# Feed-forward of a two-layer trunk: the first two feature tiles of each layer by eight plain products, their weights split ahead of the norm, a buffer for each feature tile

## The chip, the core and the metric

The kernel runs on one core of a Trainium2 chip. The metric is device time in microseconds of one execution, the median over runs. The engines are named as in the profile: PE (TensorE matmul), PEld (TensorE weight load), DVE (VectorE), ACT (ScalarE), POOL (GpSimd), SP (SyncE, which issues the loads spoken of here).

## The reference, cut to what matters

The program is one inference step of a two-layer trunk over 640 tokens of width 1024 (128 context tokens and 512 latent ones). Layer 0 mixes by attention and a state-space scan, layer 1 by an RWKV-7 scan. Behind each mixer stands the same feed-forward, which the change is about:

```
h = modulate(rmsnorm(x, P['norm_ffn_g'][layer]), sh2, sc2)
x = x + gt2 * swiglu(h, P['ffn_w_gate'][layer], P['ffn_w_up'][layer], P['ffn_w_down'][layer])
```

with `swiglu(h, wg, wu, wd) = (silu(h @ wg) * (h @ wu)) @ wd`. The hidden width is 2816, that is 22 feature tiles of 128. All of it is float32. The modulation (`sh2`, `sc2`, `gt2`) comes from a product of the condition vector with `mod_w`, which the kernel calls ada.

## The kernel before, in words

Both feed-forwards are made by one function, `ffn(layer, todo, keep, after)`. Tokens lie along the free axis, in two halves of 320; the width of 1024 lies on the partitions, in 8 blocks `k`.

**Precision.** Every product is made from operands split in a high part (a rounded cast, made on ACT) and a low part (the difference, made on DVE or POOL), by three matmuls: high by high, high by low, low by high. `operand(src)` splits 512 columns of weights: `S.copy` at L968 (tile `oh`), the subtraction on DVE at L969 (tile `ol`). Eight buffers of each are there.

**Seven products in place of eight.** For one feature tile, gate and up (2) by the two halves of the width (2) by the two halves of the tokens (2) would be 8 block products of 4 k-blocks, that is 12 matmuls of 128x320 each. The kernel uses a scheme with 7 (`PRODUCTS`), whose inputs are sums: on the side of the activations B11, B21, B22 and T1 to T4 (`sums`, each split in two steps of 640 columns), on the side of the weights four sums for each feature tile, made on POOL (`blocks`, L986, L987, L989, L991). Two feature tiles go together, a pair, so a pair has 2 x 7 x 12 = 168 matmuls (`product`, L1000). `collect` takes the results out of PSUM, adds, applies Silu and, in `to_hidden`, splits the hidden tile into `hid` (cast on ACT at L1009, low part on POOL at L1010).

**Order of the work.** The feature tiles go in groups of 4, 6, 6 and 6 (`GROUPS`). Behind each group come its down products (`down_step`, L1080). Ahead of the first pair stand the loads of its weights (SP), the splits of what is ready of them, two ada steps (`steps(jobs, 2)`: a load of 512 KB and 8 small matmuls each, L235), the sums of squares of the norm (L333), an inverse square root in 11 small DVE instructions (L117 to L123) and its spread over the partitions (`npr`, L347). Then `normed` makes h chunk by chunk (DVE at L1043, ACT at L1045). Within the first pair, each product is preceded by the making of its input.

**Memory.** All inputs h and later all hidden tiles share one buffer of 30,720 bytes a partition (`ip`, tag `hid`). Raw weights (6 of 4,096 bytes, shared with the ada loads), `oh` and `ol` (8 of 2,048 each) lie right behind it. A pool opened over memory that an earlier stage used waits, tile by tile, for the last use of what lay there. Ahead of the feed-forward of layer 0 stands the output projection (L401), whose weights take the first 36,864 bytes of this region and whose split inputs `mh` and `ml` the next 40,960; ahead of that of layer 1 stands the projection with `rwkv_w_o` (L1840). The order of instructions on an engine is made by a scheduler at build time, from the order in the program and its own estimates; on the chip each engine takes its instructions strictly in that order.

Of the kernel before, what the change touches and what calls it, by code (L numbers as in the profile page):

```python
# [18 lines left out]
NT = 640  # L19
# [69 lines left out]
def _build(ctx, tc, I, O):  # L89
# [863 lines left out]
    def ffn(layer, todo=(), keep=None, after=None):  # L953
        with ExitStack() as st, ExitStack() as hst:
            x = X[0]
            ip = pool(st, f"if{layer}")
            wp = pool(st, f"wf{layer}", 8)
            sqp = pool(st, f"sf{layer}", 10)
            pg = pool(st, f"pfg{layer}", 2, PSUM)
            pd = pool(st, f"pfd{layer}", 6, PSUM)  # L960
            jobs = [ada(l, p, wp, pg, "wr", 6, pg, "g") for l, p in todo]
            hf = ip.tile([128, 12, NT], F32, name="hf", tag="hid")

            def operand(src):

                hi = wp.tile([128, 512], F32R, name="oh", tag="oh")
                lo = wp.tile([128, 512], F32R, name="ol", tag="ol")
                S.copy(hi, src)  # L968
                V.tensor_tensor(out=lo, in0=src, in1=hi.bitcast(F32), op=ALU.subtract)  # L969
                return hi, lo  # L970

            def raw():
                return wp.tile([128, 1024], F32, name="wr", tag="wr", bufs=6)

            def blocks(f):
# [9 lines left out]
                g3 = wp.tile([128, 512], F32, name="g3", tag="g3", bufs=2)  # L985
                G.tensor_tensor(out=g3, in0=a11, in1=a21, op=ALU.add)  # L986
                G.tensor_tensor(out=a21, in0=a21, in1=a22, op=ALU.add)  # L987
                yield operand(a21)
                G.tensor_tensor(out=a11, in0=a11, in1=a21, op=ALU.add)  # L989
                yield operand(a11)  # L990
                G.tensor_tensor(out=a12, in0=a12, in1=a11, op=ALU.add)  # L991
                yield operand(a12)
                yield operand(g3)
                yield operand(a22)
# [8 lines left out]
            def piece():  # L1003
                return sqp.tile([128, 320], F32, name="e", tag="e")

            def to_hidden(e, slot, t0):

                hi, lo = hid[:, 2 * slot, t0:t0 + 320], hid[:, 2 * slot + 1, t0:t0 + 320]
                S.copy(hi, e)  # L1009
                G.tensor_tensor(out=lo, in0=e, in1=hi.bitcast(F32), op=ALU.subtract)  # L1010

            def collect(i, bank, e, slot):

                if i in (0, 2, 3):
                    e[i] = piece()
                    S.copy(e[i], bank[:, 0:320])
                elif i == 1:
                    e[1] = piece()
                    V.tensor_tensor(out=e[1], in0=bank[:, 0:320], in1=e[0], op=ALU.add)
                    S.activation(e[1], e[1], AF.Silu)  # L1020
                elif i == 4:
                    V.tensor_tensor(out=e[3], in0=bank[:, 0:320], in1=e[3], op=ALU.add)
                    S.activation(e[3], e[3], AF.Silu)
                else:
# [3 lines left out]
                    to_hidden(up, slot, 320 if i == 5 else 0)  # L1028
# [6 lines left out]
            H = {n: [hop.tile([128, 4, 320], F32R, name=n + z) for z in "hl"] for n, _, _ in PRODUCTS}  # L1035
            h = {f"B{a + 1}{b + 1}": hf[:, 4 * a:4 * a + 4, b * 320:b * 320 + 320] for a in range(2) for b in range(2)}
            h['T1'] = h['T3'] = hf[:, 8:10].rearrange("p a (b t) -> p (a b) t", b=2)
            h['T2'] = h['T4'] = hf[:, 10:12].rearrange("p a (b t) -> p (a b) t", b=2)

            def normed(a, half):  # L1040
                for k in range(4 * a, 4 * a + 4):
                    for v, c0, c1 in ((1, 320, 640),) if half else ((0, 0, 128), (1, 128, 320)):
                        V.scalar_tensor_tensor(out=hf[:, k, c0:c1], in0=x[:, k, c0:c1], scalar=ag[:, layer * 2 + 1, v, k:k + 1],  # L1043
                                               in1=rstd[v][:, c0 - 128 * v:c1 - 128 * v], op0=ALU.mult, op1=ALU.mult)
                        S.activation(hf[:, k, c0:c1], hf[:, k, c0:c1], AF.Identity, bias=mod[:, layer, v, 24 + k:25 + k])  # L1045

            def sums(n):

                if n in ('B11', 'B21'):
                    normed(n == 'B21', 0)  # L1050
                elif n in ('T1', 'T2'):
                    normed(n == 'T2', 1)
                for j in range(0, 4, 2):
                    js = slice(j, j + 2)
                    o = h[n][:, js]
                    if n == 'T1':
                        V.tensor_tensor(out=o, in0=h['B11'][:, js], in1=h['B12'][:, js], op=ALU.subtract)
                    elif n == 'T2':
                        V.scalar_tensor_tensor(out=o, in0=h['T1'][:, js], scalar=-1.0, in1=h['B22'][:, js], op0=ALU.mult, op1=ALU.subtract)
                    elif n == 'T3':  # L1060
                        V.tensor_tensor(out=o, in0=h['B22'][:, js], in1=h['B12'][:, js], op=ALU.subtract)
                    elif n == 'T4':
                        V.scalar_tensor_tensor(out=o, in0=h['T2'][:, js], scalar=-1.0, in1=h['B21'][:, js], op0=ALU.mult, op1=ALU.subtract)
                    S.copy(H[n][0][:, js], o)
                    (G if j else V).tensor_tensor(out=H[n][1][:, js], in0=o, in1=H[n][0][:, js].bitcast(F32), op=ALU.subtract)

            def down_blocks(f0, f1, q):

# [6 lines left out]

            def down_step(bank, c0, c1, ops, m, i, n):
                w = [o[:, (m % 4) * 128:(m % 4) * 128 + 128] for o in ops[i]]
                a = [hid[:, 2 * i + z, c0:c1] for z in range(2)]
                for z, (p, q) in enumerate(((w[0], a[0]), (w[0], a[1]), (w[1], a[0]))):
                    T.matmul(bank[:, 0:c1 - c0], p, q, start=i == 0 and z == 0, stop=i == n - 1 and z == 2)  # L1080

            for gi, (f0, f1) in enumerate(GROUPS):
                n = f1 - f0
                for fp in range(f0, f1, 2):
                    gens = first if fp == 0 else [blocks(f) for f in (fp, fp + 1)]
                    banks, es = [{}, {}], [{}, {}]
                    for i, (hn, b, start) in enumerate(PRODUCTS):
                        ops = early[i] if fp == 0 and i < 2 else [next(g) for g in gens]
                        if fp == 0 and i < 6:
                            sums(hn)  # L1090
                            if i == 5:
                                sums('T4')
                                hid = ip.tile([128, 12, NT], F32R, name="hid", tag="hid")
# [812 lines left out]
```

## Time and profile before

| | us |
|---|---|
| median of 3 runs | 2154.29 |
| lowest and highest run | 2151.95, 2156.15 |
| profiled execution, its own time | 2159.76 |
| its span, first to last instruction | 2158.0 |
| PE busy in the span | 1965.2 (91%) |
| DVE, ACT, POOL busy | 1461.4, 947.4, 684.1 |
| feed-forward of layer 0: first product, first product of the second pair | at 456.25, at 497.55 |
| feed-forward of layer 1: the same | at 1692.78, at 1733.88 |

The profiled execution was 5.5 us longer than the median of the runs. Its span leaves out 1.8 us around it. The mean granted clock of TensorE in the span was 0.934.

### The profile page before, as it was taken

To read this page: it belongs to the slowest core of one execution; us is meant where nothing else is said; L and a number is where in the kernel's file an instruction comes from. 1 tells how busy PE (TensorE), PEld (TensorE's weight loads), DVE (VectorE), ACT (ScalarE), POOL (GpSimd) and SP (SyncE) were. 2 spreads that over 40 slices of the span, in tenths; PEclk is the share of its full clock that TensorE was granted. 3 is DMA by queue.
4 is the path that set the end of the run, shared out by engine and by line. 5 is a ranking of instruction groups with operands and counts; after the bars stand their busy time and mean duration, and the time that the engine had idled before them with its cause. 6 is when DMAs were issued, how large, how long until landed. Compare 5 with 4: busy or idle time off the path is not lost. (4 is left out here: it accounts for less than half of the span.)

```text
span 2158.0 us, 42969 instructions
## 1 busy us (share of the span) xinstructions
PE 1965.2 (91%) x17653; PEld 1791.4 (83%) x17653; DVE 1461.4 (68%) x2527; ACT 947.4 (44%) x1738; POOL 684.1 (32%) x596
## 2 busy tenths in 40 slices
PE   7999988978999999989999897877889699999998
PEld 6887776968999999969676786866778589999998
DVE  4474675377665757587676839989766876666575
ACT  4333454253443524356555243544553634444351
POOL 2112231044442426131144123314231545345340
PEclk8999899979999999989997988878789799999999
DMA  8663001134342424242466635434243242223221
GB/s 293 212 214 99 3 1 40 40 117 128 94 151 79 148 65 131 105 131 64 129 220 211 214 100 140 123 90 148 81 148 92 85 127 78 81 63 113 59 89 50
DMA packets 256408, 245.73 MB, mean 114 GB/s; under 512 B 27849, under 2 KB 217298, under 8 KB 256084
## 3 DMA queue, kind: packets, MB, share of 16 engines
q1 hardware_dynamic: 233076, 208.87, 32.1%
q0 software_dynamic: 5856, 21.01, 3.0%
q10 hardware_dynamic: 17280, 13.11, 2.0%
q8 instruction: 139, 2.28, 0.5%
q14 instruction: 57, 0.47, 0.1%
HBM read 203.76 MB, written 39.19 MB: 113 GB/s over the span
## 5 line engine op out<-in xcount | busy, mean ns | idle before, releaser
L969 DVE TENSOR_TENSOR ol<-wr,oh 128x512 fp32r<-128x512 f32 x352 | 344.0, 991 | 110.6 <-ACT oh L968 101.3
L968 ACT CAST oh<-wr 128x512 fp32r<-128x512 f32 x352 | 216.4, 619 | 327.8 <-PE d L1080 187.5
L1080 PE MATMUL d<-hid,oh 128*128 128x320 f32 x1312 | 290.6, 310 | 5.4 <-POOL hid L1010 5.4
L1080 PEld LDWEIGHTS d<-hid,oh 128*128 128x128 f32 x1312 | 220.5, 189 | 5.9 <-POOL hid L1010 5.9
L1080 PE MATMUL d<-hid,ol 128*128 128x320 f32 x656 | 203.4, 310 | 0.0
L443 DVE SCALAR_TENSOR_TENSOR x<-d,mod,x 128x128 f32<-128x128 f32 (+2 forms) x204 | 77.3, 434 | 167.5 <-PE d L1080 133.3
L1010 POOL TENSOR_TENSOR hid<-e,hid 128x320 fp32r<-128x320 f32 x88 | 102.1, 1174 | 141.7 <-ACT hid L1009 138.7
L986 POOL TENSOR_TENSOR g<-wr 128x512 f32<-128x512 f32 x44 | 62.8, 1427 | 261.9 <-DMA wr<-in_ffn_w_up_dram 222.1
L401 PE MATMUL d<-hh,wh 128*128 128x320 f32 (+1 forms) x464 | 119.0, 328 | 6.2 <-ACT hh L435 3.6
L1080 PEld LDWEIGHTS d<-hid,ol 128*128 128x128 f32 x656 | 123.8, 189 | 0.0
L401 PE MATMUL d<-hl,wh 128*128 128x320 f32 (+1 forms) x464 | 115.4, 320 | 3.9 <-POOL hl L436 3.9
L401 PE MATMUL d<-hh,wl 128*128 128x320 f32 (+1 forms) x464 | 114.1, 318 | 0.6 <-DVE wl L388 0.6
L388 DVE TENSOR_TENSOR wl<-wr,wh 128x1024 fp32r<-128x1024 f32 (+1 forms) x57 | 70.6, 1239 | 55.2 <-ACT wh L386 54.7
L386 ACT CAST wh<-wr 128x1024 fp32r<-128x1024 f32 (+1 forms) x57 | 58.7, 1034 | 104.3 <-PE d L401 71.7
L401 PEld LDWEIGHTS d<-hh,wh 128*128 128x128 f32 (+1 forms) x464 | 79.9, 191 | 20.8 <-ACT hh L435 5.0
L989 POOL TENSOR_TENSOR wr<-wr 128x512 f32<-128x512 f32 x44 | 63.5, 1446 | 82.7 <-DVE ol L969 57.2
L1009 ACT CAST hid<-e 128x320 fp32r<-128x320 f32 x88 | 40.5, 460 | 110.0 <-DVE e L1027 109.8
L991 POOL TENSOR_TENSOR wr<-wr 128x512 f32<-128x512 f32 x44 | 67.9, 1554 | 63.7 <-DVE ol L969 63.6
L401 PEld LDWEIGHTS d<-hl,wh 128*128 128x128 f32 (+1 forms) x464 | 80.3, 191 | 7.7 <-POOL hl L436 5.2
L401 PEld LDWEIGHTS d<-hh,wl 128*128 128x128 f32 (+1 forms) x464 | 80.2, 191 | 2.7 <-DVE wl L388 1.2
L1489 PE MATMUL pS<-ar,ta 64*128 64x128 f32 x640 | 57.1, 314 | 19.6 <-POOL uv L1557 7.6
L1489 PEld LDWEIGHTS pS<-ar,ta 64*128 64x128 f32 x640 | 49.2, 216 | 26.8 <-POOL ar L1476 8.9
(606 smaller groups left out, 6037.2 us busy)
## 6 DMA issues: line engine op xcount, KB each, us to landing
wt<-in_mod_w_dram SPq DMA_DIRECT2D x80, 512.0 KB, 4.4
wr<-in_ffn_w_gate_dram SPq DMA_DIRECT2D x44, 512.0 KB, 4.0
wr<-in_ffn_w_up_dram SPq DMA_DIRECT2D x44, 512.0 KB, 4.6
wr<-in_ffn_w_down_dram SPq DMA_DIRECT2D x44, 512.0 KB, 4.5
ta<-kbd SPq DMA_DIRECT2D x10, 1024.0 KB, 6.5
ar<-rkd SPq DMA_DIRECT2D x20, 512.0 KB, 6.3
wr<-in_ab_w_in_dram SPq DMA_DIRECT2D x16, 512.0 KB, 8.5
wt<-in_mod_w_dram SPq DMA_DIRECT2D x6, 1024.0 KB, 10.5
```

Of the source, the lines that this page charges most:

```text
L386: S.copy(wh, wr)
L388: V.tensor_sub(wl, wr, wh.bitcast(F32))
L401: T.matmul(ps[b][0:cn, 0:320], w[:, k, 0:cn], a[:, t0:t1], start=(k == 0 and i == 0), stop=(k == w.shape[1] - 1 and i == 2))
L443: V.scalar_tensor_tensor(out=x[:, k, c0:c1], in0=ps[b][:, c0 - 320 * b:c1 - 320 * b], scalar=mod[:, layer, v, gcol + k:gcol + k + 1], in1= ...
L968: S.copy(hi, src)
L969: V.tensor_tensor(out=lo, in0=src, in1=hi.bitcast(F32), op=ALU.subtract)
L986: G.tensor_tensor(out=g3, in0=a11, in1=a21, op=ALU.add)
L989: G.tensor_tensor(out=a11, in0=a11, in1=a21, op=ALU.add)
L991: G.tensor_tensor(out=a12, in0=a12, in1=a11, op=ALU.add)
L1010: G.tensor_tensor(out=lo, in0=e, in1=hi.bitcast(F32), op=ALU.subtract)
L1080: T.matmul(bank[:, 0:c1 - c0], p, q, start=i == 0 and z == 0, stop=i == n - 1 and z == 2)
L1489: T.matmul(pS[i][:, m], bk[r, g4 * 4 + m, :], ar[r, g4 * 4 + m], start=True, stop=True)
```

## The change

For feature tiles 0 and 1 of each layer the eight plain block products take the place of the seven: no sums of weights are needed, and no T1 to T4. So all eight weight operands of the two tiles are split before the norm. The products run k by k: as soon as one block of 320 tokens is normed and split (`normed`, `part_of`), its matmuls follow (`plain_step`); first the first half of the tokens for both tiles, then the second half. T1 to T4 are made behind that, for the later pairs. The second pair (tiles 2 and 3) makes its weight sums on DVE in place of POOL, and the last pair of each group makes the low parts of its hidden tiles on DVE in place of POOL. The one buffer for h and hidden tiles becomes six of [128, 4, 320]; some of the H tiles, the raw weights and the operands get places of their own, in another order of pools in each layer. Four ada steps stand in the first pair (two behind each half) where three stood.

```diff
-            ip = pool(st, f"if{layer}")
+            if layer == 0:
+                ip, sqp = pool(st, "if0", 6), pool(st, "sf0", 11)
+                hops.update(dict.fromkeys(('B11', 'B21', 'T1'), pool(st, "hf0a")))
+                gp, wrp = pool(st, "gf0", 2), pool(st, "wr0", 6)
+            else:
+                wrp, ip, sqp = pool(st, "wr1", 6), pool(st, "if1", 6), pool(st, "sf1", 11)
+                hops.update(dict.fromkeys(('B22', 'T2', 'T3', 'T4'), pool(st, "hf1a")))
+                gp = pool(st, "gf1", 2)
             wp = pool(st, f"wf{layer}", 8)
-            sqp = pool(st, f"sf{layer}", 10)
...
+                if plain:
+                    yield operand(a21)
+                    yield operand(a22)
+                    return
...
-            first = [blocks(f) for f in (0, 1)]
-            early = [[next(g) for g in first] for _ in range(2)]
+            first = [list(blocks(f, True)) for f in (0, 1)]
             steps(jobs, 2)
             rstd = norm_spread(norm_rstd(pg, sqp), pd, "d")
...
+            for half in range(2):
+                at = [('B11', 'B21'), ('T4', 'B22')][half]
+                ps = [[pd.tile([128, 512], F32, name="d", tag="d") for _ in range(2)] for f in range(2)]
+
+                def plain_step(f, k):
+                    for i in range(2):
+                        w, a = first[f][2 * i + k // 4], H[at[k // 4]]
+                        jw = slice((k % 4) * 128, (k % 4) * 128 + 128)
+                        for z, (p, q) in enumerate(((w[0], a[0]), (w[0], a[1]), (w[1], a[0]))):
+                            T.matmul(ps[f][i][:, 0:320], p[:, jw], q[:, k % 4], start=k == 0 and z == 0, stop=k == 7 and z == 2)
+
+                for k in range(8):
+                    n = f"B{1 + k // 4}{1 + half}"
+                    normed(n, k % 4)
+                    part_of(n, slice(k % 4, k % 4 + 1), at[k // 4])
+                    plain_step(0, k)
+                    if not half:
+                        plain_step(1, k)
+                if half:
+                    for k in range(8):
+                        plain_step(1, k)
+                for f in range(2):
+                    e = piece()
+                    S.activation(e, ps[f][0][:, 0:320], AF.Silu)
+                    V.tensor_tensor(out=e, in0=ps[f][1][:, 0:320], in1=e, op=ALU.mult)
+                    to_hidden(e, f, half, V)
+                steps(jobs, 2)
+            for n in ('T1', 'T2', 'T3', 'T4'):
+                sums(n)
...
-                for fp in range(f0, f1, 2):
-                    gens = first if fp == 0 else [blocks(f) for f in (fp, fp + 1)]
+                for fp in range(max(f0, 2), f1, 2):
+                    gens = [blocks(f, E=V if fp == 2 else G) for f in (fp, fp + 1)]
...
-                            collect(i, banks[z][b], es[z], fp - f0 + z)
+                            collect(i, banks[z][b], es[z], fp + z, V if fp + 2 == f1 else G)
```

`part_of(n, js)` casts a piece of h to the high part on ACT and subtracts on DVE; `sums(n)` makes one of T1 to T4 on DVE in two steps of 640 columns and calls it for each.

## Rows read from the trace of the kernel before

**Rows 1.** The page: busy us of each engine and its share.

```profile
PE 1965.2 (91%) x17653; PEld 1791.4 (83%) x17653; DVE 1461.4 (68%) x2527; ACT 947.4 (44%) x1738; POOL 684.1 (32%) x596
```

**Rows 2.** The chain that ended last, a piece of it: start us, us, what.

```profile
1910.32 74.00 PE d L1000 x504
```

**Rows 3.** Stretches: length; busy us (instructions) PE, PEld, DVE, ACT, POOL; clock, DMA.

```profile
434.14:456.25 22.11, 11.11 (x65) 8.01 (x65) 16.69 (x35) 8.64 (x20) 12.53 (x8) 0.61 0.48 141
456.25:497.55 41.30, 33.98 (x177) 30.48 (x177) 36.74 (x45) 27.62 (x55) 23.47 (x15) 0.83 0.30 87
497.55:524.71 27.16, 27.16 (x196) 25.34 (x195) 22.69 (x35) 13.91 (x29) 10.03 (x9) 1.00 0.58 177
524.71:555.70 30.99, 28.41 (x194) 28.15 (x193) 17.79 (x33) 5.79 (x10) 12.57 (x10) 1.00 0.11 34
...
1672.10:1692.78 20.68, 9.01 (x66) 6.64 (x65) 15.61 (x34) 8.16 (x19) 10.04 (x7) 0.67 0.33 103
1692.78:1733.88 41.10, 34.33 (x177) 29.50 (x177) 36.52 (x45) 27.52 (x55) 23.52 (x14) 0.83 0.29 87
...
1761.15:1793.93 32.78, 29.95 (x194) 29.68 (x193) 18.19 (x33) 5.79 (x10) 12.84 (x11) 0.95 0.11 30
```

**Rows 4.** PE in order of time ahead of the first product, layer 0, then layer 1.

```profile
439.74 1.08 PE L235 MATMUL pa<-wt,sT 128*32 128x256 f32 x8 [5.61 <-DMA wt<-in_mod_w_dram]
...
451.18 2.47 PE L347 MATMUL npr<-ca,rs 128*128 128x128 f32 x10 [4.57 <-DVE rs L123]
...
1675.21 0.64 PE L235 MATMUL pa<-wt,sT 128*32 128x256 f32 x8 [3.11 <-DMA wt<-in_mod_w_dram]
...
1676.02 1.25 PE L333 MATMUL nps<-ca,acc 128*128 128x1 f32 x10
1677.14 2.27 PE L333 MATMUL nps<-ca,sq 128*128 128x1 f32 x10
...
1687.71 2.48 PE L347 MATMUL npr<-ca,rs 128*128 128x128 f32 x10 [7.29 <-DVE rs L123]
```

**Rows 5.** DVE in order of time ahead of the first product, layer 0.

```profile
445.39 2.88 DVE L969 TENSOR_TENSOR ol<-wr,oh 128x512 fp32r<-128x512 f32 x2 [1.81 <-ACT oh L968]
448.20 0.15 DVE L117 TENSOR_SCALAR rq_v<-nps 128x5 f32<-128x5 f32 x1
...
453.70 2.49 DVE L1043 SCALAR_TENSOR_TENSOR hf<-x,ag,npr 128x192 f32<-128x192 f32 x8 [0.84 <-PE npr L347]
```

**Rows 6.** SP: issues of the first weight loads, layer 0 (first, last) and layer 1.

```profile
427.13 0.37 SPq L103 DMA_DIRECT2D wr<-in_ffn_w_gate_dram  x1
...
433.29 0.37 SPq L103 DMA_DIRECT2D wr<-in_ffn_w_up_dram  x1
...
1663.51 0.37 SPq L103 DMA_DIRECT2D wr<-in_ffn_w_gate_dram  x1
```

**Rows 7.** ACT in order of time ahead of the first product, layer 0.

```profile
444.74 1.14 ACT L968 CAST oh<-wr 128x512 fp32r<-128x512 f32 x2 [5.92 <-POOL wr L987]
...
454.14 1.44 ACT L1045 ACTIVATE hf<-hf,mod 128x192 f32<-128x192 f32 x4 [0.79 <-DVE hf L1043]
```

**Rows 8.** Groups by line: weight splits without POOL beside them, in the first pair; copies there.

```profile
L969 DVE TENSOR_TENSOR ol<-wr,oh 128x512 fp32r<-128x512 f32 x3 | 2.1, 694 | 0.1
...
L969 DVE TENSOR_TENSOR ol<-wr,oh 128x512 fp32r<-128x512 f32 x7 | 10.1, 1457 | 0.0
...
L1016 ACT COPY e<-d 128x320 f32<-128x320 f32 x6 | 2.6, 428 | 5.7 <-PE d L1000 5.7
```

**Rows 9.** PE in order of time at the first down products, layers 0 and 1.

```profile
531.11 0.41 PE L1080 MATMUL d<-hid,oh 128*128 128x320 f32 x1 [2.58 <-POOL hid L1010]
...
1767.81 0.42 PE L1080 MATMUL d<-hid,oh 128*128 128x320 f32 x1 [2.83 <-POOL hid L1010]
```

**Rows 10.** PE in order of time in the first pair, at the low clock.

```profile
478.06 0.47 PE L1000 MATMUL d<-T2l,oh 128*128 128x320 f32 x1
478.33 0.47 PE L1000 MATMUL d<-T2h,ol 128*128 128x320 f32 x1
```

More of the change, by code (lines that the diff above doesn't have):

```diff
@@ L955, in ffn, with hid_tile @@
             x = X[0]
-            ip = pool(st, f"if{layer}")
+            hops = {}
+            if layer == 0:
[6 more added lines that the diff above has]
+                gp = pool(st, "gf1", 2)
             wp = pool(st, f"wf{layer}", 8)
-            sqp = pool(st, f"sf{layer}", 10)
             pg = pool(st, f"pfg{layer}", 2, PSUM)
             pd = pool(st, f"pfd{layer}", 6, PSUM)
-            jobs = [ada(l, p, wp, pg, "wr", 6, pg, "g") for l, p in todo]
-            hf = ip.tile([128, 12, NT], F32, name="hf", tag="hid")
+            jobs = [ada(l, p, wrp, pg, "wr", 6, pg, "g") for l, p in todo]
+            def hid_tile(dt):
+                return ip.tile([128, 4, 320], dt, name="hid", tag="hid")
             def operand(src):
@@ L972, in raw, with blocks @@
             def raw():
-                return wp.tile([128, 1024], F32, name="wr", tag="wr", bufs=6)
-            def blocks(f):
+                return wrp.tile([128, 1024], F32, name="wr", tag="wr")
+            def blocks(f, plain=False, E=G):
                 ws = []
@@ L984, in blocks @@
                 yield operand(a12)
-                g3 = wp.tile([128, 512], F32, name="g3", tag="g3", bufs=2)
-                G.tensor_tensor(out=g3, in0=a11, in1=a21, op=ALU.add)
-                G.tensor_tensor(out=a21, in0=a21, in1=a22, op=ALU.add)
+                if plain:
+                    yield operand(a21)
+                    yield operand(a22)
+                    return
+                g3 = gp.tile([128, 512], F32, name="g3", tag="g3")
+                E.tensor_tensor(out=g3, in0=a11, in1=a21, op=ALU.add)
+                E.tensor_tensor(out=a21, in0=a21, in1=a22, op=ALU.add)
                 yield operand(a21)
-                G.tensor_tensor(out=a11, in0=a11, in1=a21, op=ALU.add)
+                E.tensor_tensor(out=a11, in0=a11, in1=a21, op=ALU.add)
                 yield operand(a11)
-                G.tensor_tensor(out=a12, in0=a12, in1=a11, op=ALU.add)
+                E.tensor_tensor(out=a12, in0=a12, in1=a11, op=ALU.add)
                 yield operand(a12)
@@ L1004, in piece, with to_hidden, collect @@
                 return sqp.tile([128, 320], F32, name="e", tag="e")
-            def to_hidden(e, slot, t0):
-                hi, lo = hid[:, 2 * slot, t0:t0 + 320], hid[:, 2 * slot + 1, t0:t0 + 320]
+            hid = {}
+            def to_hidden(e, f, b, E):
+                if f not in hid:
+                    hid[f] = hid_tile(F32R)
+                hi, lo = hid[f][:, b], hid[f][:, 2 + b]
                 S.copy(hi, e)
-                G.tensor_tensor(out=lo, in0=e, in1=hi.bitcast(F32), op=ALU.subtract)
-            def collect(i, bank, e, slot):
+                E.tensor_tensor(out=lo, in0=e, in1=hi.bitcast(F32), op=ALU.subtract)
+            def collect(i, bank, e, f, E):
                 if i in (0, 2, 3):
@@ L1034, in ffn, with part_of, normed @@
             hop = pool(hst, f"hf{layer}", 1, side="right")
[L1035 to L1045, printed above, removed]
+            H = {n: [hops.get(n, hop).tile([128, 4, 320], F32R, name=n + z) for z in "hl"] for n, _, _ in PRODUCTS}
+            h = {n: hid_tile(F32) for n in ('B11', 'B21', 'B12', 'B22', 'T2')}
+            h.update(T1=h['B11'], T3=h['B12'], T4=h['T2'])
+            def part_of(n, js, out=None):
+                hi, lo = (z[:, js] for z in H[out or n])
+                S.copy(hi, h[n][:, js])
+                V.tensor_tensor(out=lo, in0=h[n][:, js], in1=hi.bitcast(F32), op=ALU.subtract)
+            def normed(n, j):
+                k, half = j + 4 * (n[1] == '2'), n[2] == '2'
+                for v, c0, c1 in ((1, 320, 640),) if half else ((0, 0, 128), (1, 128, 320)):
+                    o = h[n][:, j, c0 - 320 * half:c1 - 320 * half]
+                    V.scalar_tensor_tensor(out=o, in0=x[:, k, c0:c1], scalar=ag[:, layer * 2 + 1, v, k:k + 1],
+                                           in1=rstd[v][:, c0 - 128 * v:c1 - 128 * v], op0=ALU.mult, op1=ALU.mult)
+                    S.activation(o, o, AF.Identity, bias=mod[:, layer, v, 24 + k:25 + k])
             def sums(n):
[L1049 to L1052, printed above, removed]
                 for j in range(0, 4, 2):
@@ L1056, in sums @@
                     if n == 'T1':
-                        V.tensor_tensor(out=o, in0=h['B11'][:, js], in1=h['B12'][:, js], op=ALU.subtract)
+                        V.tensor_tensor(out=o, in0=o, in1=h['B12'][:, js], op=ALU.subtract)
                     elif n == 'T2':
@@ L1060, in sums @@
                     elif n == 'T3':
[L1061 to L1065, printed above, removed]
+                        V.tensor_tensor(out=o, in0=h['B22'][:, js], in1=o, op=ALU.subtract)
+                    else:
+                        V.scalar_tensor_tensor(out=o, in0=o, scalar=-1.0, in1=h['B21'][:, js], op0=ALU.mult, op1=ALU.subtract)
+                    part_of(n, js)
+            for half in range(2):
[25 more added lines that the diff above has]
+                sums(n)
             def down_blocks(f0, f1, q):
@@ L1077, in down_step @@
                 w = [o[:, (m % 4) * 128:(m % 4) * 128 + 128] for o in ops[i]]
-                a = [hid[:, 2 * i + z, c0:c1] for z in range(2)]
+                a = [hid[f0 + i][:, 2 * z:2 * z + 2].rearrange("p b t -> p (b t)")[:, c0:c1] for z in range(2)]
                 for z, (p, q) in enumerate(((w[0], a[0]), (w[0], a[1]), (w[1], a[0]))):
@@ L1083, in ffn @@
                 n = f1 - f0
-                for fp in range(f0, f1, 2):
-                    gens = first if fp == 0 else [blocks(f) for f in (fp, fp + 1)]
+                for fp in range(max(f0, 2), f1, 2):
+                    gens = [blocks(f, E=V if fp == 2 else G) for f in (fp, fp + 1)]
                     banks, es = [{}, {}], [{}, {}]
                     for i, (hn, b, start) in enumerate(PRODUCTS):
[L1088 to L1093, printed above, removed]
+                        ops = [next(g) for g in gens]
                         for z in range(2):
```

2 lines of the change are left out of this document (1 added, 1 removed).

## The prediction

> **What bounds the kernel now.** I read the page first: PE is busy for 91% of the span [rows 1], so time can only come off where PE waits, runs at the lower clock, or does less. The chain of waits then shows where it does none of the first two: most of each feed-forward is an unbroken run of products, 504 of them in 74.00 us, which makes 0.147 us a matmul of 128x320 [rows 2]. A pair of 168 is 24.7 us at that rate, and the second pair of layer 0 takes 27.16 us with its three ada steps [rows 3]: nothing is to be had there. The table of stretches says what is left. From the end of the projection to the first product PE is busy for 11.11 of 22.11 us in layer 0 and 9.01 of 20.68 us in layer 1; the first pair takes 41.30 and 41.10 us at a mean clock of 0.83; the first group of down products takes 30.99 and 32.78 us for 192 matmuls that need 28.2 [rows 3]. These three places, in two layers, are all that the change touches.
>
> Last I asked each engine what it waits for there. Ahead of the first product of layer 0, PE waits 5.61 us for the load of an ada weight and then 4.57 us for the inverse square root on DVE; in layer 1 the two waits are 3.11 and 7.29 us [rows 4]. The ada loads are late because they stand in SP's queue behind four weight loads, and those start only at 427.13 to 433.29 and at 1663.51 [rows 6], while the projection ends at 434.14 and 1672.10: their buffers lie over that projection's operands. The root is late because DVE, which takes its queue in order, has weight splits ahead of it that wait for ACT casts, which wait for sums on POOL: 5.92 us on ACT [rows 7], then two splits at 445.39 and only at 448.20 the root [rows 5]. In layer 1 PE is through with the squares at 1679.4, and the spread, which needs the root, starts at 1687.71 [rows 4].
>
> **The norm stretch.** By the sizes of the pools, the raw weights of layer 0 come to lie 79,680 bytes into the region, behind the 77,824 that the projection uses. Their loads and all eight splits can be done beside the projection, where PE alone is busy. The POOL sums are gone. PE in layer 0: projection to 434.14; two ada steps at 0.64 [rows 4] to 435.4; the accumulated squares 1.25 at the full clock, the last ones 2.27 at the half clock [rows 4], with 0.2 for the opening matmul: 439.1. The root took 2.98 from its start to the spread, the spread 2.47 [rows 4, 5]: 444.5. From the end of the spread to the first product it was 2.6 before, with four blocks and a cast of 640 columns ahead; now it is one block: DVE 0.31, ACT 0.36 [rows 5, 7], a cast near the 0.43 of a 320 copy [rows 8], 0.2 of handing on: 1.3. First product at 445.8 in place of 456.25: **10.5 us**. In layer 1 the raw weights lie over the scan's buffers and load early, but most of `oh` lies over the last projection slabs, so I let all eight splits wait for its end: 8 x 0.69 [rows 8] from about 1673.5 is 1679.0, which is later than PE's squares (1677.0). Then 2.98 + 2.48 + 1.3: 1685.7 in place of 1692.78, **7.1 us**. Bounds: 5.6 and 3.1 less if the loads still come late; 2 more in layer 1 if the splits come early.
>
> **The first pair.** It gets 24 matmuls more, 192 x 0.147 = 28.2 us, and four ada steps, 2.6. Will it be fed? A block of 320 tokens costs DVE two chunks of 0.31 and a subtraction of about 0.45 (320 columns, by the 0.69 that 512 take [rows 8]), together 1.1 us, and ACT about 1.1; its 12 matmuls take 1.76. So PE sets the pace in the first half and DVE and ACT run ahead by some 5 us for the second, where a block costs about 1.0 us for 0.88 us of the first tile's matmuls, and the second tile's 7 us follow without any need. T1 to T4 (16 DVE steps of 640 columns, about 0.86, 13.8 us) come behind that, under the second half's 14.1. The clock had a mean of 0.61 and 0.67 ahead of the first product, 0.83 in the pair and 1.00 behind it [rows 3], and at the half level a product takes 0.27 [rows 10]. I allow 4 us at the half level, which costs 2.0, and 1.5 for the first blocks and for the change of halves, where PSUM banks come free. Sum 34.3, against 41.30 and 41.10: **7.0 and 6.8 us**. Bounds: 30.8 with no such loss; with the whole first half at 0.27 (96 x 0.12 = 11.8 in place of 2.0) 44.1, a loss of 3.
>
> The Trainium skill ("TensorE: Matmul & The Clock Gate", Part 1) says that the array's default state is the throttled one and that steady work releases it. By it, matmuls added right behind a wait are the dearest in the kernel, and the first rival below is how far that could go; if both halves ran so, the pair would take about 55 us. The 0.83 of the old pair, with its waits, agrees in kind; a pair without them should come up sooner, and I stay with 4 us.
>
> **The second pair.** Its weight operands need buffers that the plain products free one by one: after the first tile's block 4 of the second half, two, some 10 us before the pair begins. DVE was busy for 22.7 of 27.2 us there [rows 3]; it gets 8 sums of 0.69 and 4 low parts of 0.5, 7.5 us, and loses the delay that POOL's work beside it gave: the same split takes 0.69 without POOL and 1.46 in the first pair with it [rows 8]. With 10.03 us of POOL work gone from that stretch I take the two as equal: 0. Bounds: 3 us a layer lost if the delay stays, 8 if T1 to T4 come late as well.
>
> **The first down products.** PE waits 2.58 and 2.83 us for a low part on POOL [rows 9], and in layer 1 the stretch falls to a clock of 0.95 [rows 3]. On DVE the low part takes 0.5 and does not queue behind POOL's sums of the next pair. From the last product it takes two DVE steps, a cast and that, 1.9 us alone and 3.3 at the slow rate; 24 matmuls cover 3.5. So the excess of 2.8 and 4.6 nearly goes: **6.5 us**. For the other groups 48 matmuls cover it already, and POOL against DVE makes no odds. If DVE is queued up: 3.
>
> **Ada.** Four steps in the first pair in place of three leave one less for later in each layer: **1.3 us**. The six buffers for hidden tiles, the extra one of 11 for `e` and the new order of pools cost nothing by themselves: hidden tile 1 may have to wait for an input tile to come free, but is read only 30 us later.
>
> **Sum.** 10.5 + 7.1 + 7.0 + 6.8 + 6.5 + 1.3 = 39.2 us. The profiled execution took 2159.76, so 2120.6; it was 5.5 above the median of the runs, and the prediction is for that: **2115**.
>
> **Rivals.** *The first half stays at the low clock.* The rows show the clock falling again within the first pair (0.83). If gaps between blocks keep it down for all 96 products, each layer loses 9.8: 2135. Against it: 12 matmuls a block on 1.1 us of supply. *The second pair runs short of operands*, DVE having T1 to T4, the sums and the low parts at once: 8 each, 2131. For it: DVE was busy for 36.7 of 41.3 us in the first pair. *The change doesn't bring the loads forward*, the scheduler leaving them behind the projection: 5.6 + 3.1 lost, 2124. *DVE becomes the bound, and the kernel is slower.* The place is from the norm to the end of the second pair. DVE had 59 us of work there [rows 3] and gets 7 subtractions at 0.86 that POOL had and 8 sums at 0.69: 71 if nothing gets faster, against 61.5 of PE. It decides from 81 us a layer, where the 39 are used up; at 85 the time is 2162. Against it: POOL has next to nothing left there.
>
> *The busiest engine's work decides.* 48 matmuls more on PE are 48 x 0.147 = 7.0 us, and if the waits only moved, the time would be 2161. The Trainium skill ("Perfetto Trace Analysis", Identifying the Most-Contended Engine) says to look to the engine with the highest occupancy first, which is PE here, and by it work should not be added there. The rows speak against it: PE is idle for 11 us ahead of each first product.
>
> **How the numbers follow.** My forecast, a gain of 30 to 48 us: 0.70. Low clock 0.08, second pair 0.09, late loads 0.08, DVE as the bound 0.03, more PE work 0.02. All but the last two are faster. A time within 0.2% (4.3 us, what a measurement of this kernel can tell from no change) fits none of them well; I leave 0.03 for it, 0.04 for slower, 0.93 for faster. Without any stall or loss of clock the gain would be 49, so 2105; above, the range takes in the late loads, the second pair and half of the low clock's cases: 2104 to 2134.
>
> **What would show it.** The first weight loads issued long before the projection's end; no wait of PE for an ada load; the first product 10.5 and 7 us earlier; 192 products in some 32 us with the clock back within the first 5; the second pair starting at 479 to 480 where it was 497.55 and taking 27 us or less; no wait for a low part at the first down products. The prediction is wrong if the product stretch shows waits for DVE, if the second pair takes over 30 us, or if the spread still waits for splits.

## The result, and the profile after

The changed kernel takes 2119.89 us (median of 4 runs, 2116.96 to 2125.63) against 2155.22 before (4 runs): a ratio of 0.9841, interval 0.9815 to 0.9866. That is 35.3 us off. The forecast was 2115, with a range of 2104 to 2134: faster, as predicted, at nearly the predicted size. Two of its terms were wrong all the same, and the experiments below are about those.

The profiled execution took 2116.96 us, the fastest of the four. The page's first row answers to [rows 1]:

```profile
PE 1950.7 (92%) x17701; PEld 1785.1 (84%) x17701; DVE 1447.0 (68%) x2589; ACT 940.2 (44%) x1734; POOL 560.6 (27%) x510
```

PE has 48 matmuls more and is busy for 14.5 us less; the mean granted clock of the span is 0.943 where it was 0.934. The table of stretches, cut at the same four places as [rows 3] (end of the projection, first product, second pair, first down product, next pair), layer 0 and then layer 1; columns as there:

```profile
429.14:439.37 10.23, 8.46 (x82) 5.46 (x81) 5.55 (x24) 3.26 (x10) 0.00 (x0) 0.83 0.83 222
439.37:475.83 36.46, 33.59 (x219) 32.12 (x219) 26.78 (x55) 22.55 (x52) 0.00 (x0) 0.91 0.19 68
475.83:501.62 25.79, 24.90 (x170) 24.64 (x169) 24.75 (x42) 16.44 (x33) 2.62 (x2) 1.00 0.45 123
501.62:533.67 32.05, 30.30 (x194) 29.64 (x193) 20.08 (x38) 5.97 (x11) 8.43 (x7) 0.95 0.11 34
1645.53:1658.54 13.01, 10.77 (x80) 6.44 (x80) 10.32 (x31) 7.34 (x18) 0.00 (x0) 0.61 0.76 232
1658.54:1692.81 34.27, 31.62 (x216) 30.69 (x213) 26.40 (x55) 22.27 (x52) 0.00 (x0) 0.95 0.30 96
1692.81:1718.60 25.79, 24.90 (x170) 24.64 (x169) 24.75 (x42) 16.48 (x33) 2.53 (x2) 1.00 0.44 123
1718.60:1749.60 31.00, 29.13 (x195) 28.25 (x194) 20.11 (x38) 5.99 (x11) 8.85 (x7) 1.00 0.12 35
sum 208.60, PE 193.67 PEld 181.88 DVE 158.75 ACT 100.29 POOL 22.43; mean PE 24.21 PEld 22.73 DVE 19.84 ACT 12.54 POOL 2.80
```

The same eight stretches took 243.4 us before, so they give 34.8 of the 35.3. The spans of the two profiled executions differ by 8 us more; that lies outside these stages (5.0 ahead of layer 0's, 4.5 between the layers, 1.5 the other way behind), and in the runs below these outer parts moved by about as much from one execution to the next. Set beside the forecast, in us saved over both layers:

| term | forecast | measured |
|---|---|---|
| norm stretch | 10.5 + 7.1 = 17.6 | 11.9 + 7.7 = 19.6 |
| first pair | 7.0 + 6.8 = 13.8 | 4.8 + 6.8 = 11.6 |
| second pair, with the ada term | 1.3 | 1.4 + 1.5 = 2.9 |
| first down products | 6.5 | -1.1 + 1.8 = 0.7 |
| sum | 39.2 | 34.8 |

**Norm stretch.** The loads and PE in order of time, layer 0 (SP's first issue of a feed-forward weight and its last of an ada weight there, then PE), which answer to [rows 6] and [rows 4]; the last two rows are PE in layer 1:

```profile
369.58 0.71 SPq L103 DMA_DIRECT2D wr<-in_ffn_w_gate_dram  x1
...
391.05 1.81 SPq L103 DMA_DIRECT2D wt<-in_mod_w_dram  x2
...
430.47 1.25 PE L333 MATMUL nps<-ca,acc 128*128 128x1 f32 x10
431.59 1.25 PE L333 MATMUL nps<-ca,sq 128*128 128x1 f32 x10
432.77 3.60 PE L235 MATMUL pa<-wt,sT 128*32 128x256 f32 x32
436.30 1.38 PE L347 MATMUL npr<-ca,rs 128*128 128x128 f32 x10
439.37 1.25 PE L1096 MATMUL d<-B11h,oh 128*128 128x320 f32 x4 [1.69 <-ACT B11h L1060]
...
1652.60 1.08 PE L235 MATMUL pa<-wt,sT 128*32 128x256 f32 x8 [1.56 <-DMA wt<-in_mod_w_dram]
1654.09 2.48 PE L347 MATMUL npr<-ca,rs 128*128 128x128 f32 x10 [0.41 <-DVE rs L123]
```

The first weight load is issued 60 us before the projection ends at 429.14, where it was 7 us [rows 3, 6]. In layer 0 no wait for an ada load is left, and the wait for the root has gone: four ada steps fill it. Their loads still stand behind the four weight loads in SP's queue, but that whole queue is now issued ahead of the projection's end. The spread took 1.38, where [rows 4] had 2.47. In layer 1 a wait of 1.56 us for an ada load is left, in time in which the root is not ready either, then 0.41 for the root, and 0.27 for another ada load just ahead of the first product; the spread takes 2.48.

**Change of halves.** PE at the end of the first half of the first pair, layer 0 and layer 1:

```profile
455.18 1.07 PE L235 MATMUL pa<-wt,sT 128*32 128x256 f32 x16
456.80 0.44 PE L243 MATMUL pm<-ca,mr 128*128 128x128 f32 x2 [0.55 <-DVE mr L240]
459.56 0.64 PE L235 MATMUL pa<-wt,sT 128*32 128x256 f32 x8 [2.32 <-DMA wt<-in_mod_w_dram]
...
1677.09 0.85 PE L1096 MATMUL d<-T4h,oh 128*128 128x320 f32 x4 [2.10 <-ACT T4h L1060]
```

The last product of the first half ends near 455.2, and the first of the second starts at 460.13: 4.88 us without one, 4.21 in layer 1. `T4h` holds the high part of the second half's first inputs here. Behind the gap come products at 0.27 us each, the half level, and the second half's 96 products take 15.7 us in both layers in place of 14.1. DVE at that place, layer 0, and ACT's first cast for the second half:

```profile
454.48 0.49 DVE L1111 TENSOR_TENSOR e<-d,e 128x320 f32<-128x320 f32 x1 [6.62 <-ACT e L1110]
455.36 0.49 DVE L1111 TENSOR_TENSOR e<-d,e 128x320 f32<-128x320 f32 x1 [0.39 <-ACT e L1110]
456.32 0.42 DVE L240 COPY mr<-pa 128x256 f32<-128x256 f32 x1 [0.47 <-PE pa L235]
456.66 0.88 DVE L1028 TENSOR_TENSOR hid<-e,hid 128x320 fp32r<-128x320 f32 x2
457.46 1.92 DVE L1067 SCALAR_TENSOR_TENSOR hid<-x,ag,npr 128x320 f32<-128x320 f32 x4
...
458.96 0.80 ACT L1060 CAST T4h<-hid 128x320 fp32r<-128x320 f32 x2
```

DVE has nothing to do for 6.62 us. Then it collects the first half's result into the two hidden tiles (L1111, L1028), and only behind that makes the first input of the second half (L1067). It did not run ahead. In layer 1 PE starts 0.5 us behind the start of the first cast of `T4h`, for which it waits. In layer 0 that cast starts at 458.96 and PE at 460.13, so of layer 0's gap the ada step of 459.56 can account for some 0.7 us at most.

**First down products.** PE, then DVE and POOL just before, layer 0; [rows 9] is the place before:

```profile
506.55 0.41 PE L1130 MATMUL d<-hid,oh 128*128 128x320 f32 x1 [1.25 <-ACT hid L1027]
507.46 0.41 PE L1130 MATMUL d<-hid,oh 128*128 128x320 f32 x1 [0.50 <-DVE hid L1028]
...
499.12 1.59 DVE L1045 SCALAR_TENSOR_TENSOR e<-e 128x320 f32<-128x320 f32 x1
500.63 1.77 DVE L979 TENSOR_TENSOR ol<-wr,oh 128x512 fp32r<-128x512 f32 x1
502.32 1.57 DVE L1028 TENSOR_TENSOR hid<-e,hid 128x320 fp32r<-128x320 f32 x1
...
504.22 1.38 DVE L979 TENSOR_TENSOR ol<-wr,oh 128x512 fp32r<-128x512 f32 x1
...
498.92 1.43 POOL L1000 TENSOR_TENSOR g<-wr 128x512 f32<-128x512 f32 x1 [142.84 <-DVE e L1044]
500.43 1.42 POOL L1001 TENSOR_TENSOR wr<-wr 128x512 f32<-128x512 f32 x1
502.23 1.32 POOL L1000 TENSOR_TENSOR g<-wr 128x512 f32<-128x512 f32 x1 [0.38 <-DMA wr<-in_ffn_w_up_dram]
```

The low part is on DVE now, but POOL's sums for the next pair run at the same moment: three DVE steps that take 0.48 to 0.69 elsewhere take 1.6 to 1.8, and a weight split of the next pair (L979, at 504.22) takes 1.38 between the last steps of the hidden tiles.

### The profile page after: what moved, and what is told of

Its sections match the earlier page's. It is cut to its first block, busy times and chain, and to the rows that moved or that the text cites. A ratio compares the mean times of both kernels' runs of the same rounds, so it can differ in the third digit from the quotient of the medians.

```text
span 2115.2 us, 42931 instructions
## 1 busy us (share of the span) xinstructions
PE 1950.7 (92%) x17701; PEld 1785.1 (84%) x17701; DVE 1447.0 (68%) x2589; ACT 940.2 (44%) x1734; POOL 560.6 (27%) x510
## 5 line engine op out<-in xcount | busy, mean ns | idle before, releaser
L979 DVE TENSOR_TENSOR ol<-wr,oh 128x512 fp32r<-128x512 f32 x344 | 316.1, 935 | 101.0 <-ACT oh L978 93.6
L978 ACT CAST oh<-wr 128x512 fp32r<-128x512 f32 x344 | 211.3, 619 | 307.1 <-PE d L1130 174.7
L1000 POOL TENSOR_TENSOR g<-wr 128x512 f32<-128x512 f32 x36 | 48.4, 1344 | 460.0 <-DMA wr<-in_ffn_w_up_dram 280.8
L1003 POOL TENSOR_TENSOR wr<-wr 128x512 f32<-128x512 f32 x36 | 50.6, 1409 | 84.9 <-DVE ol L979 57.0
L1005 POOL TENSOR_TENSOR wr<-wr 128x512 f32<-128x512 f32 x36 | 53.3, 1492 | 66.4 <-DVE ol L979 66.4
L1562 DVE TENSOR_TENSOR xt__11664<-ta 128x31 f32<-128x31 f32 (+15 forms) x155 | 66.4, 429 | 4.4 <-ACT ta L1760 0.2
```

The costliest lines, as they stand in the source:

```text
L1003: E.tensor_tensor(out=a11, in0=a11, in1=a21, op=ALU.add)
L1005: E.tensor_tensor(out=a12, in0=a12, in1=a11, op=ALU.add)
L1562: V.tensor_tensor(out=tv, in0=nu[:, j + 1:32, j:j + 1].to_broadcast([128, n, j + 1]), in1=wu[:, j:j + 1, 0:j + 1].to_broadcast([128, n, j ...
```

## The experiments

Eight changes start from the kernel after, or put part of it back; one (places alone) starts from the kernel before. All ratios are against the kernel before, run beside them on the same chip. "Stages" is the sum over the eight stretches of the one profiled execution, 208.6 in the kernel after and 243.4 before. For differences of a few us the readings rest on the stretches, since the intervals of the times overlap.

**All inputs ahead of the collecting** (the order of the instructions in the first pair).

```
+ def inputs(half, k): normed(n, k % 4); part_of(n, ...)
  for k in range(8):
-     normed(n, k % 4); part_of(n, ...)
+     if not half: inputs(0, k)
      plain_step(0, k)
...
+ if not half:
+     for k in range(8): inputs(1, k)
  for f in range(2):   # collecting
```

> Only the order in the program changes: the normed and split inputs of the second half of the tokens are made ahead of the collecting of the first half. Theory (buffers are handed out in the order of the program, so that the inputs of the second half waited for hidden tiles 0 and 1 to be given theirs): DVE and ACT run ahead while PE is in the first half, the idle time of PE between the halves (4.95 us from 455.18 to 460.13 in layer 0, 4.27 us in layer 1, ada steps within) falls to the ada steps alone, some 1 to 2 us, and the low clock behind it (1.7 us) goes; the first pair falls from 36.5 and 34.3 us to 31 to 33, the whole by 6 to 10 us. Rival (the change of halves waits for PSUM banks or for ada loads, whatever the order): the first pair stays within 1 us of 36.5 and 34.3.

Measured: 2103.98 us, ratio 0.9771 (0.9747 to 0.9796), stages 192.6. The first pair is at the full rate in both layers (its stretches, layer 0 and layer 1):

```profile
438.07:466.33 28.26, 28.25 (x192) 28.25 (x193) 27.80 (x57) 23.26 (x52) 0.00 (x0) 1.00 0.08 31
...
1650.96:1679.22 28.26, 28.26 (x192) 28.26 (x193) 27.82 (x56) 23.24 (x52) 0.00 (x0) 1.00 0.27 79
```

192 products in 28.26 us are 0.147 each [rows 2]: no gap and no loss of clock is left. So DVE and ACT can feed this pair, and the order kept them from it.

**No ada between the halves**, the rival for the gap, since PE's row names an ada load.

```
- steps(jobs, 2)
+ if half: steps(jobs, 4)
```

> The two ada steps between the halves are moved behind the second half. Theory of the buffers: the first block of the second half is ready at the same time as before, so PE's idle stretch between the halves stays at 4 to 5 us in both layers, only with less in it. Rival (the ada load that ended PE's wait of 2.32 us in layer 0 sets the time): the stretch between the halves falls by 2 us or more in layer 0.

Measured, one run: 2118.7 us, stages 207.8. The gap stays, 5.61 and 4.21 us, and in layer 0 PE shows the same wait:

```profile
459.71 1.08 PE L235 MATMUL pa<-wt,sT 128*32 128x256 f32 x8 [2.61 <-DMA wt<-in_mod_w_dram]
```

The instructions of the change of halves asked for no ada step here; the scheduler filled the hole with one all the same, so in layer 0 this run does not take the rival away. Layer 1 speaks against it: there PE waits 2.10 us for `T4h`, in the kernel after and in this run, with no ada load in between. The next run settles it.

**Early use of two buffers**: what in the order matters? Nothing is moved here; one column of two input tiles is written ahead of the loop.

```
+ for n in ('B12', 'B22'):
+     V.memset(h[n][:, 0, 0:1], 0.0)
  for half in range(2):
```

> The kernel after, with one column of the two input tiles of the second half (B12, B22) set to zero by DVE ahead of the first half's loop; the instructions of the loop itself stand as in the kernel after. The columns are overwritten later, so the output does not change. Theory (buffers: tiles of one pool get their slots in the order of first use, so in the kernel after the two hidden tiles of the first half come ahead of B12 and B22, and the second half's inputs can't be placed before the collecting): with the early use B12 and B22 have their slots first, the second half's inputs run under the first half's products, the gap between the halves falls from 4.9 and 4.2 us to under 1 us, the first pair to 28 to 30 us in both layers, and the time to 2102 to 2109. Rival (order of the instructions: the queues follow the order in which the instructions are written down, and the slots have no part in it): the gap stays at 4 to 5 us, the first pair at 34 to 36.5 us and the time at 2116 to 2124.

Measured: 2104.23 us (2100.94 to 2106.38), ratio 0.9774 (0.9744 to 0.9804), stages 192.6, the first pair 28.27 and 28.26. The rival fell, and so did the one of the ada load: the ada steps stand in the program where they stood, and the gap is gone. DVE in order of time, layer 0:

```profile
448.17 0.54 DVE L1067 SCALAR_TENSOR_TENSOR hid<-x,ag,npr 128x320 f32<-128x320 f32 x1
...
457.35 0.89 DVE L1113 TENSOR_TENSOR e<-d,e 128x320 f32<-128x320 f32 x2
```

The second half's inputs now start at 448.17, 9.2 us before the collecting, although the code has them behind it. Input tiles and hidden tiles come from one pool of six; the run bears out that its slots go out in the order of first use. In the kernel after, hidden tiles 0 and 1 are used first, by the collecting, so B12 and B22 have no slot until it stands in the schedule, and DVE's queue follows; how the scheduler keeps its slots was not looked at beyond this. Two writes of one column are worth 16.0 us of stages: 14.2 in the first pair and 3.4 in the first down products, less 2.0 in the second pair, where the ada steps now run.

**Low part on POOL again**, the rest as after.

```
- collect(i, banks[z][b], es[z], fp + z, V if fp + 2 == f1 else G)
+ collect(i, banks[z][b], es[z], fp + z, G)
```

> The low parts of the hidden tiles of each group's last pair go back to POOL. The prediction had 6.5 us for their move to DVE; the trace of the changed kernel shows the first down products no faster (32.05 and 31.00 us, against 30.99 and 32.78 before). If the move brings nothing, since DVE is slowed by POOL's sums of the next pair and has splits queued between, the two stretches stay within 1.5 us of 32.05 and 31.00 and PE's wait is for POOL again, of 2 to 3 us. If the move did bring what was predicted and something else took it, they grow by 3 us each.

Measured: 2123.17 us, ratio 0.9853 (0.9827 to 0.9879), stages 212.3. The first down products take 33.08 and 34.33 against 32.05 and 31.00, with a wait longer than that of [rows 9]:

```profile
507.12 0.63 PE L1130 MATMUL d<-hid,oh 128*128 128x320 f32 x1 [3.13 <-POOL hid L1028]
```

Layer 0 is within the 1.5 us for a move that brings nothing, layer 1 beyond the 3 for one that brings what was forecast. So the move does bring something, 1.0 + 3.3 = 4.3 us in this stage; without the ada steps between the halves, a change that does not touch this stage, it took 32.40 and 31.90, so that some 1.2 us of this is uncertain. But with the old placing the stage would have been 2.1 and 1.5 us longer than before the change, and that took most of it back. The second pair ends 1.4 us sooner per layer than before, while DVE is busy for 24.75 of its 25.79 us; that its work therefore lies closer to the down products fits, but was not tried by itself. The two runs that mend the first pair point the same way: in layer 0 the second pair then takes 27.16 us, with ada steps in it, and the down products take 29.23, although POOL's sums still run beside them.

**Sums of the next pair on DVE**, so that POOL does nothing beside the first down products.

```
- gens = [blocks(f, E=V if fp == 2 else G) for f in (fp, fp + 1)]
+ gens = [blocks(f, E=V if fp in (2, 4) else G) for f in (fp, fp + 1)]
```

> The weight sums of the third pair (tiles 4 and 5), which POOL makes at the time of the last collecting of the first group, are made on DVE too, so that POOL does nothing there. Theory (POOL's sums slow the DVE steps of that chain to 1.6 us from 0.5 to 0.7): no DVE step above 0.9 us there, PE's waits of 1.75 and 1.87 us at the first down products fall below 0.7 and the low clock behind it goes; the stretch falls from 32.05 and 31.00 to about 28.5 to 30, the whole by 3 to 5 us. Rival (the weight splits queued between the steps of the chain hold it): the waits stay above 1.3 us, and the sums on DVE may add to them.

Measured: 2115.29 us, ratio 0.9815 (0.9794 to 0.9837), stages 203.2. Second pair and first down products, layer 0 and layer 1:

```profile
475.90:502.56 26.66, 25.15 (x170) 24.65 (x169) 24.92 (x46) 16.65 (x33) 0.00 (x0) 1.00 0.44 121
502.56:530.72 28.16, 28.16 (x195) 28.16 (x193) 19.23 (x43) 5.87 (x10) 0.00 (x0) 1.00 0.11 37
...
1694.67:1721.42 26.75, 25.14 (x170) 24.64 (x169) 24.91 (x46) 16.68 (x33) 0.00 (x0) 1.00 0.43 120
1721.42:1749.58 28.16, 28.16 (x195) 28.16 (x193) 19.34 (x43) 5.89 (x10) 0.00 (x0) 1.00 0.13 37
```

28.16 is 192 x 0.147: no wait at all. No DVE step there is above 0.7 us until the sums are done. It gives 3.9 and 2.8 us there and costs 0.9 and 1.0 in the second pair. DVE has more to do and is done sooner, since four of its steps beside POOL's sums had cost 0.7 to 1.1 us more each. The Trainium skill ("SBUF — State Buffer", Who interferes with whom) says that a DVE instruction with two SBUF inputs contends with a GpSimd instruction that reads SBUF; the steps of 1.57 to 1.77 beside POOL's sums and this run's 28.16 without them agree.

**Sums of the second pair on POOL**, as before the change.

```
- gens = [blocks(f, E=V if fp == 2 else G) for f in (fp, fp + 1)]
+ gens = [blocks(f, E=G) for f in (fp, fp + 1)]
```

> The changed kernel with the weight sums of the second pair on POOL, as before the change. The prediction put their move to DVE at nothing. If that holds, the second pair stays within 1 us of 25.8 us in both layers. If DVE was relieved of the delay beside POOL by more than it took on, the second pair grows by 2 us or more, with DVE steps of 1.2 us and above in it; if the sums were a burden on DVE, it falls by the 0.9 us that PE waits for a split there.

Measured, one run: 2121.95 us, stages 214.1. The second pair takes 27.81 and 28.91 us against 25.79 twice; in layer 0 PE waits 2.07 and 0.56 us there for weight splits, where it waited 0.89:

```profile
476.38:504.19 27.81, 25.18 (x171) 24.65 (x169) 25.34 (x39) 15.96 (x33) 8.76 (x6) 1.00 0.39 114
...
1697.13:1726.04 28.91, 26.70 (x171) 26.17 (x169) 25.63 (x38) 15.67 (x31) 9.99 (x7) 0.94 0.40 110
```

The stages say 5.1 us for the move of these sums. The time of a single run, 2 us above the median after, can't confirm it.

**Old places**: the kernel after with its pools in the old order.

```
- ip, sqp = pool("if0", 6), pool("sf0", 11); ...; gp, wrp = ...
+ ip, wrp = pool(f"if{layer}", 6), pool(f"wr{layer}", 6)
+ wp, gp = pool(f"wf{layer}", 8), pool(f"gf{layer}", 2)
+ sqp = pool(f"sf{layer}", 11)
```

> The changed kernel with its pools in the order that the kernel before had (inputs and hidden tiles, then raw weights and operands right behind them, all inputs of the products on the far side), everything else as changed. Theory (the new places are what brings the loads ahead of the projection's end): the first weight loads are issued in the last 10 us of the projection again, PE waits for ada loads, and the stretch from the projection's end to the first product grows from 10.2 and 13.0 us to 15 to 17 in both layers, not to the 22.1 and 20.7 of before, since the sums on POOL are gone; the whole is 8 to 12 us longer than the changed kernel. Rival (the loads would come early anyhow): both stretches stay within 1.5 us.

Measured: 2133.91 us, ratio 0.9916 (0.9893 to 0.9939), stages 217.6. The norm stretches take 17.96 and 14.78 us in place of 10.23 and 13.01, the first weight load of layer 0 is issued at 422.25, 7 us before that projection's end, and the wait for the ada load is back to what [rows 4] had, in both layers:

```profile
434.63 1.08 PE L235 MATMUL pa<-wt,sT 128*32 128x256 f32 x8 [5.37 <-DMA wt<-in_mod_w_dram]
...
1663.36 0.64 PE L235 MATMUL pa<-wt,sT 128*32 128x256 f32 x8 [3.38 <-DMA wt<-in_mod_w_dram]
```

The spans of the two profiled executions differ by 17.1 us. The stages account for 9.0 of them; the other 8.1 lie between the layers, where this execution took 1120.0 us against 1111.9, and were not traced further.

**Places alone**: the kernel before with nothing but the pools in the new order.

```
+ ip, sqp = pool("if0"), pool("sf0", 10); gp, wrp = pool("gf0", 2), pool("wr0", 6)
...
- return wp.tile([128, 1024], F32, name="wr", tag="wr", bufs=6)
+ return wrp.tile([128, 1024], F32, name="wr", tag="wr", bufs=6)
```

> The kernel before with only the new places of its pools: seven products in the first pair, all sums on POOL, one buffer for inputs and hidden tiles. Theory (the gain ahead of the first product comes from the places, that within the first pair from the plain products): the stretch ahead of the first product falls from 22.1 and 20.7 us to 10 to 15, the first pair stays at 40 to 42 us, the whole is 14 to 22 us faster than the kernel before. Rival (the sums on POOL hold the root on DVE wherever the loads are): the stretch falls by less than 6 us.

Measured: 2144.69 us, ratio 0.9958 (0.9944 to 0.9972), stages 234.8: 8.0 us, less than the theory wanted. The norm stretches take 14.59 and 19.45 against 22.11 and 20.68 [rows 3], so the theory holds in layer 0 and its rival in layer 1. The first pair stays at 40.61 and 42.60 us, so what it gained comes from the plain products. PE's wait for the root is still there:

```profile
441.25 2.48 PE L347 MATMUL npr<-ca,rs 128*128 128x128 f32 x10 [3.95 <-DVE rs L123]
...
1674.26 2.48 PE L347 MATMUL npr<-ca,rs 128*128 128x128 f32 x10 [5.81 <-DVE rs L123]
```

DVE shows why. In layer 1 the splits still begin only at the end of the projection, and POOL's sums run beside them:

```profile
1660.57 6.24 DVE L976 TENSOR_TENSOR ol<-wr,oh 128x512 fp32r<-128x512 f32 x4
```

That is 1.56 a split against 0.69 [rows 8]. So the places give 7.5 + 1.2 = 8.7 us of norm. From the other side, the old-places run has 4.2 + 5.9 = 10.1 us without the places. The two add to 18.8 of the 19.6 measured. In the 10.1 stand the missing sums and the shorter way from the spread to the first product (1.69 us for 2.60 in layer 0); they were not tried apart.

**Both mends together**: all inputs first, and the sums of the next pair on DVE.

> The changed kernel with both edits that paid: the inputs of the second half ahead of the collecting of the first, and the sums of the third pair on DVE. Theory: the gains add, since they lie in different stretches: first pair 28.3 us, second pair 26.5 to 27.5, first down products 28.2, in both layers; the whole at 2098 to 2104 us, ratio to the kernel before 0.974 to 0.977. Rival (with the second half early, DVE is too full for more sums): the second pair grows above 28 us and eats what the down products give.

Measured: 2101.89 us (5 runs, 2098.38 to 2103.58), ratio 0.9759 (0.9738 to 0.9780), stages 189.8, the fastest of all. First pair and first down products, layer 0 (28.61 and 28.16 in layer 1):

```profile
441.96:470.22 28.26, 28.26 (x193) 28.26 (x193) 27.82 (x56) 23.25 (x52) 0.00 (x0) 1.00 0.07 26
...
497.38:525.54 28.16, 28.16 (x195) 28.16 (x193) 18.88 (x41) 5.80 (x10) 0.00 (x0) 1.00 0.11 36
```

Beyond the first mend alone it is 2.9 us better in the stages; in the times the intervals overlap.

## Why the prediction was right, and where it was not

**The norm stretch held**: 19.6 for 17.6. Loads ahead of the projection's end and the splits of layer 1 behind it (DVE from 1646.2 to 1651.6, the root next) came as worked out; the waits for ada loads went in layer 0 and were covered by the root, all but 0.27 us, in layer 1. Of the 2 us more, 1.4 lie in layer 0 and are a price at the wrong level: I took the last squares at 2.27 and the spread at 2.47, the half clock, and they ran at 1.25 and 1.38, with no wait ahead of the squares and ada steps in the wait ahead of the spread. In layer 1, with waits of 1.56 and 0.41 us ahead of it, the spread took 2.48. Old places and places alone show that the term is made of two nearly equal parts, the places and the rest of the change.

**The first pair failed at one step**: "PE sets the pace in the first half and DVE and ACT run ahead by some 5 us for the second." The supply was priced rightly, since 28.26 us were reached as soon as the slots allowed it. What I passed over was in the same text: the six buffers "cost nothing by themselves". I asked whether a hidden tile would wait for an input tile, and not whether an input tile would wait for a hidden one. That cost 4.9 + 4.2 us of gap and some 1.6 us of clock in the second half of each layer. Another 1.5 us of clock went in the first half of layer 0, ahead of the gap; three runs with the same order, no ada between, low part on POOL and sums on DVE, have none of it there, so it is not put down to the slots. The first of the prediction's own signs of being wrong came with the gap: the product stretch waits, and behind it stands DVE. The sum came near only since I had allowed 3.5 us a layer for other losses, and 2.6 for ada steps of which most ran in the norm stretch or in the gap. In layer 1 the forecast of 6.8 was met to the tenth, for the wrong reasons, which is luck. The size of the mistake is the 14 us by which the first pair is shorter in the two runs that remove the gap (16.0 over all stages), not the 2.2 in the table.

**The second pair** was put at nothing, with the sums' price and POOL's delay taken as equal. They are not: on POOL the sums cost 2.0 and 3.1 us more. That the stretch shrank all the same, by 1.4 and 1.5, is the work of the three ada steps that are no longer in it: 1.9 by [rows 4]'s 0.64. Without them it grew by some 0.5, and PE waits 0.89 us for a weight split there in each layer.

**The first down products failed**: 6.5 forecast, 0.7 measured. The step "the low part takes 0.5 and does not queue behind POOL's sums" is true of its queue and not of its time. The sums slow DVE steps ahead of the low part (1.4 to 1.8 us for 0.5 to 0.7), splits of the next pair stand between, and PE waits 1.25 and 0.50 us in layer 0 where it had waited 2.58. The profile before had the row for it: splits of 1.457 beside POOL [rows 8]. I used it for the second pair and not here, beyond one "3.3 at the slow rate" that I held to be covered by 24 matmuls. With POOL idle the stage is 28.16 us, so the whole excess was to be had, by moving the sums too. In layer 0 most of it also goes with the gap of the first pair mended and POOL's sums left as they are (29.23): the slow steps hurt where DVE is late already.

**The rivals.** DVE as the bound did not come: the first pair holds 26.78 us of DVE work in 36.46. It is near, though: 24.75 of 25.79 us in the second pair, and 27.80 of 28.26 in the first with the gap gone. More PE work decided nothing. The second pair did not run short, the loads did come early, and the clock of the first pair was 0.91 and 0.95, above the 0.83 before and not at the low level. The clock fell behind gaps and not with the added products: in the two runs that only remove the gap the pair's granted clock is 1.00. It did not fall behind every gap: layer 1 of the run with no ada between the halves has its gap of 4.21 us and a granted clock of 1.00. The Trainium skill ("TensorE: Matmul & The Clock Gate", Part 1) says that the throttled state is the default and that activity releases it; the 1.00 of a pair without a wait agrees.

## What to carry to other kernels

When tiles of different roles share a pool, write down the order in which they are first used: a tile late in that order can't be prepared early, however idle the engines are, and a look at the queue of the idle engine shows it. When a step is moved off a shared engine to be out of a queue, move what runs beside it as well, or price it at the slow rate of its neighbours. A stall that PE's row blames on a transfer can be a filler in someone else's gap; look at when the next product's own input is ready before believing it.

## What was not expected of the hardware

DVE finished sooner with more work: the sums cost it 0.69 each, and beside POOL steps of 0.48 to 0.69 had taken 1.57 to 1.77. PE's busy time fell by 14.5 us with 48 matmuls more. And ada steps of 32 small matmuls (3.60 us) in the wait ahead of the spread went with a spread of 1.38 in place of 2.47: they ended 1.1 us behind the root, at 436.37, and the spread took 1.1 us less, so that work of no urgency in a wait cost nothing.
